# A fused block on one core: state space matrices kept to each group's 16 channels, their matmuls as pairs of 64x64 quadrants, and fold blocks formed two steps ahead

## The chip, the core and the metric

The kernel runs on one core of a Trainium2 chip. The metric is the device time of one execution in microseconds (us). The engines are named as the profile names them: PE (TensorE matmuls) and PEld (its weight loads), DVE (VectorE), ACT (ScalarE), POOL (GpSimd) and SP (SyncE), which issues the large loads.

## The reference, cut to what matters

Two transformer blocks run one after the other on 256 tokens of width 1024 (the second block puts 16 meta tokens ahead of them). The change touches only the state space branch of the second block (32 groups, each with 64 complex states and 16 channels), and one small preparation for the memory branch beside it:

```python
u32 = u.reshape(bn, L, SSM_GROUPS, SSM_GROUP)              # 32 groups of 16 channels
lam = lax.complex(a_re, a_im); dt = jnp.exp(log_dt)[:, None]
a_bar = jnp.exp(lam * dt)                                  # (32, 64)
b_bar = ((a_bar - 1.0) / lam)[..., None] * lax.complex(b_re, b_im)   # (32, 64, 16)
bu = jnp.einsum('blgc,gpc->blgp', u32, b_bar)
_, states = lax.associative_scan(combine, (a_seq, bu), axis=1)
y = jnp.real(jnp.einsum('blgp,gcp->blgc', states, c)) + d * u32
# memory branch: q, k, v = block-diagonal 4x4 maps of xc and xm, then
gates = jnp.concatenate([q, k, v], axis=-1) @ w_if + b_if
```

## The kernel before, in words

The weights come in 468 units of 512 KB (eight tiles of 128x128). SP loads a unit into one of four buffers `wr`; ACT rounds it to `wh` (L339) and DVE forms the rest `wl` (L340), up to three units ahead of PE. PE then does three fast matmuls a tile (`mm3`, L409 to L411). A step of the first block's feed-forward layer, `up(i)` and `down(i)`, takes three units. Its product of gate and value runs on POOL (L1927) after ACT and DVE have filtered what `up(i)` left in PSUM (L1923 to L1926).

Beside that stream run generators (`K.bg`). At each new unit `tick` lets every generator go one step, as far as its credit lasts. So a step that a generator yields costs one unit of the stream, whatever it holds. The scheduler then puts each engine's instructions in order; `K.paced()` lets an instruction of POOL come only after the newest feed-forward product.

`_prep` is such a generator, and runs during the feed-forward layer. It prepares the state space branch in chunks of four time steps:

- `paced` forms the matrices `bx`, `c0` and `cx` on POOL, with complex multiplications of six operations each (L577). There are eight of them: three for `bx`, one for `c0`, four for `cx`. Groups stand in pairs `q` (16 of them), 64 states of each on a half of the partitions. Each matrix has 32 columns a time step, of which a group uses its own 16 and the other 16 are zero.
- `inputs` turns `bx` into `ew` on PE (`pt`, L606), 4 at a time, copied by ACT (L607). It multiplies `bx` by `c0` into `pk` (L614), adds the direct term `d` on DVE (L620, L621), and puts the blocks of the result at their places in `tz` with ten small transfers that ACT issues (L626).
- After the powers of `a_bar` (DVE, L564 to L569) comes the fold: for each `e` in 8, POOL forms three blocks in the one buffer `ex` (`expand`, L504), and one step later PE multiplies them by the gate weights (`pf`, L657).

`_block2` runs the branch: `us` is written to DRAM and read back as `u4` with four transfers (L746), `pe` multiplies it by `ew` (L755), DVE scans, `py` forms the outputs from `tz`, `u4`, `cx` and `z2` (L793, L795), and the result goes through DRAM again (L804, four transfers). All of these matmuls are in plain float32: one such instruction leaves two records in the trace.

Of the kernel before, what the change touches and what calls it, by code (L numbers as in the profile page):

```python
# [18 lines left out]
P = 128  # L19
# [145 lines left out]
def _s5_layout(one):  # L165

    lam = np.stack([one("ssm_a_re_2"), one("ssm_a_im_2"), np.repeat(one("ssm_log_dt_2")[:, None], 64, 1)])
    lam = lam.reshape(3, 16, P).transpose(2, 0, 1).reshape(P, 48)
    bp, cp = np.zeros((P, 2, 16, 32), np.float32), np.zeros((P, 2, 16, 32), np.float32)
    for i, z in enumerate(("re", "im")):  # L170
        b, c = one(f"ssm_b_{z}_2"), one(f"ssm_c_{z}_2")
        for g in range(32):
            q, e = g // 2, g % 2
            bp[e * 64:(e + 1) * 64, i, q, e * 16:(e + 1) * 16] = b[g]
            cp[e * 64:(e + 1) * 64, i, q, e * 16:(e + 1) * 16] = c[g].T
    d = np.tile(one("ssm_d_2").reshape(16, 32).T, (4, 1))
    return np.concatenate([lam, bp.reshape(P, -1), cp.reshape(P, -1), d], 1)
# [302 lines left out]
def _prep(K, dump):  # L480
# [6 lines left out]
    ew = EW.a(16, 2, P)  # L487
    cx = [CX.a(16, 4, 32) for _ in range(2)]
    tz = TT.a(16, P)
# [19 lines left out]
    raw = ZZ.t[:, 0:2112]  # L509
    nc.scalar.dma_start(raw, I["s5p"])  # L510
    lr, li, ld = raw[:, 0:16], raw[:, 16:32], raw[:, 32:48]
    B = raw[:, 48:1072].rearrange("p (a b c) -> p a b c", a=2, b=16)
    C = raw[:, 1072:2096].rearrange("p (a b c) -> p a b c", a=2, b=16)
    dd = raw[:, 2096:2112]
    nc0, dk = (raw[:, 48 + 512 * i:560 + 512 * i].rearrange("p (a b) -> p a b", a=16) for i in range(2))
    x1, x2, kk = (ZZ.t[:, 2112 + 512 * i:2624 + 512 * i].rearrange("p (a b) -> p a b", a=16) for i in range(3))
    c0 = [TT.t[:, 2048 + 512 * i:2560 + 512 * i].rearrange("p (a b) -> p a b", a=16) for i in range(2)]
    sc = TT.t[:, 3568:4096].rearrange("p (a b) -> p a b", b=16)
    bx = [BX.a(16, 4, 32) for _ in range(2)]
# [51 lines left out]
    def paced(dr, di, xr_, xi, yr, yi):  # L571

        ops = []
        cmul(dr, di, xr_, xi, yr, yi, x1, x2, lambda *z: ops.append(z))
        for n, z in enumerate(ops):
            with K.paced():
                g.tensor_tensor(*z)  # L577
            if n not in (0, 3):
                yield 0.1

    bc = lambda z: _bc(z, 2, 32)
# [18 lines left out]
    def inputs():  # L600

        for i in range(2):
            for q4 in range(4):
                pt = K.ps("pt")
                for j in range(4):
                    tp(pt[:, j * P:(j + 1) * P], bx[i][:, 4 * q4 + j].rearrange("p a b -> p (a b)"), K.ident)  # L606
                nc.scalar.copy(ew[:, 4 * q4:4 * q4 + 4, i], pt.rearrange("p (a b) -> p a b", a=4))  # L607
                yield 0.1

        pk = K.ps("pk")  # L610
        for q in range(16):
            o = pk[:, q * 32:q * 32 + 32]
            for i in range(2):
                mm(o, bx[i][:, q].rearrange("p a b -> p (a b)"), (c0[0], nc0)[i][:, q], start=i == 0, stop=i == 1)  # L614
            if q % 4 == 3 and q < 15:
                yield 0.1
        nc.scalar.copy(kk, pk.rearrange("p (a b) -> p a b", a=16))
        yield 0.1
        lo = slice(96, 128)
        tt(dk[lo], _bc(K.ident[lo, 96:128], 1, 16), _bc(dd[lo], 2, 32), ALU.mult)  # L620
        tt(kk[lo], kk[lo], dk[lo], ALU.add)  # L621
        yield 1.2
        for t in range(4):
# [38 lines left out]
def _block2(K, X, eps, dump, stop):  # L662
# [62 lines left out]
    for n in range(4):  # L725
# [7 lines left out]
        if n >= 2:  # L733
# [3 lines left out]
            wait = []  # L737
    def ssm():
# [1271 lines left out]
```

## Time and profile before

| | |
|---|---|
| three runs, median | 1557.08 us (1553.6 to 1557.94) |
| profiled execution, its own time | 1555.69 us |
| its span in the trace | 1553.9 us |
| PE busy | 1523.9 us, 98% of the span |
| DVE, ACT, POOL busy | 1163.0, 832.5, 250.5 us |
| mean granted PE clock | 0.994 |
| HBM traffic | 164 GB/s over the span |

The span runs from the first to the last instruction that the profiler saw; 1.8 us of the execution's own time lie outside it. A busy PE is a PE with at least one matmul in flight, since matmuls overlap; how long a group of them holds the stream is read from the starts of what stands ahead of it and behind it. A granted clock of 1.00 is 2.4 GHz, and a matmul stream at the lower level runs at 1.2 GHz.

### The profile page before, as it was taken

The numbers are of one execution on the slowest core, as the hardware profiler recorded it, in microseconds if no ns is written. First come the engines' busy times: TensorE is split into PE (matmuls) and PEld (weight loads), VectorE is DVE, ScalarE is ACT, GpSimd is POOL, SyncE is SP. The second block draws the span as 40 slices with busy tenths as digits, with TensorE's granted clock in tenths as the row PEclk, the third lists the DMA queues.
The fourth block names the chain that finished last, engine by engine and source line by source line (L and its number), as shares of the span: only waits on it lengthen the run. The fifth ranks groups of instructions, "written<-read, shape, count | busy, mean of one in ns | idle before, by whom it ended". The sixth has DMA issues, their size and how long they took to land.

```text
span 1553.9 us, 29821 instructions
## 1 busy us (share of the span) xinstructions
PE 1523.9 (98%) x11693; PEld 1416.5 (91%) x11693; DVE 1163.0 (75%) x2168; ACT 832.5 (54%) x1441; POOL 250.5 (16%) x255
## 2 busy tenths in 40 slices
PE   9999999999989999999999999999999999999998
PEld 7999899999979988989999999999999888888886
DVE  6765667897866698478999888888999666665664
ACT  7764355764435557565454554554445555555554
POOL 1000000189641010001101520112222000000000
PEclk9999999999989999999999999999999999999999
DMA  7543245554545453346455455445545666656653
GB/s 269 162 136 124 96 135 186 190 186 156 153 147 164 137 162 127 105 136 207 146 177 190 151 176 189 156 160 162 163 163 165 201 193 195 195 191 192 197 194 110
DMA packets 81149, 258.09 MB, mean 166 GB/s; under 512 B 17520, under 2 KB 19312, under 8 KB 80752
## 3 DMA queue, kind: packets, MB, share of 16 engines
q1 hardware_dynamic: 69344, 247.32, 49.3%
q10 hardware_dynamic: 11664, 8.86, 1.9%
q8 instruction: 92, 1.51, 0.4%
q14 instruction: 49, 0.40, 0.1%
HBM read 253.36 MB, written 2.13 MB: 164 GB/s over the span
## 4 chain that ended last, share of the span: by engine, by line
PE 78%; DVE 11%; POOL 4%; issue 2%; ACT 2%; DMA 1%; SPq 0%; ACTq 0%; DVEq 0%; POOLq 0%
PE acc L1316 22%; PE U L409 6%; PE U L411 6%; PE U L410 6%; DVE wl L340 5%; PE g L409 3%; PE g L411 3%; PE g L410 3%; PE pG L1196 2%; POOL s L577 2%; DVE s L771 1%; PE u L409 1%; PE u L410 1%; PE u L411 1%; ACT wh L339 1%
## 5 line engine op out<-in xcount | busy, mean ns | idle before, releaser
L340 DVE TENSOR_TENSOR wl<-wr,wh 128x1024 fp32r<-128x1024 f32 (+1 forms) x469 | 595.2, 1272 | 199.5 <-ACT wh L339 196.2
L339 ACT CAST wh<-wr 128x1024 fp32r<-128x1024 f32 (+1 forms) x469 | 490.4, 1048 | 394.7 <-PE U L410 156.0
L1316 PE MATMUL acc<-wh,wring 128*128 128x512 f32 x1024 | 315.5, 389 | 0.0
L409 PE MATMUL U<-hh,wh 128*128 128x256 f32 x1024 | 292.5, 286 | 0.0
L411 PE MATMUL U<-hh,wl 128*128 128x256 f32 x1024 | 288.1, 281 | 1.5 <-DVE wl L340 1.4
L410 PE MATMUL U<-hl,wh 128*128 128x256 f32 x1024 | 288.3, 282 | 0.0
L1316 PEld LDWEIGHTS acc<-wh,wring 128*128 128x128 f32 x1024 | 192.2, 188 | 39.8
L1316 PE MATMUL acc<-wl,wring 128*128 128x512 f32 x512 | 199.2, 389 | 0.0
L411 PEld LDWEIGHTS U<-hh,wl 128*128 128x128 f32 x1024 | 193.9, 189 | 1.9 <-DVE wl L340 1.9
L409 PEld LDWEIGHTS U<-hh,wh 128*128 128x128 f32 x1024 | 193.4, 189 | 0.0
L410 PEld LDWEIGHTS U<-hl,wh 128*128 128x128 f32 x1024 | 192.5, 188 | 0.0
L1307 ACT ACTIVATE wring<-act 128x256 fp32r<-128x256 f32 x128 | 53.3, 418 | 150.5 <-PE acc L1316 147.0
L1316 PEld LDWEIGHTS acc<-wl,wring 128*128 128x128 f32 x512 | 96.1, 188 | 20.0
L1308 DVE SCALAR_TENSOR_TENSOR wring<-act,wring 128x256 fp32r<-128x256 f32 x128 | 54.7, 428 | 60.7 <-PE acc L1316 58.7
L409 PE MATMUL u<-hh,wh 128*128 128x256 f32 x320 | 92.4, 290 | 1.4 <-DVE ffn L1925 1.2
L411 PE MATMUL u<-hh,wl 128*128 128x256 f32 x320 | 91.4, 287 | 0.8 <-DVE wl L340 0.8
L410 PE MATMUL u<-hl,wh 128*128 128x256 f32 x320 | 91.4, 287 | 0.0
L1277 POOL TENSOR_TENSOR act<-act,ga 128x16 f32<-128x16 f32 (+31 forms) x77 | 56.1, 728 | 212.8 <-ACT ga L1276 190.2
L456 POOL TENSOR_TENSOR sq<-sq,sq 128x256 f32<-128x256 f32 x18 | 16.0, 888 | 402.6 <-ACT sq L452 402.4
L409 PE MATMUL g<-hh,wh 128*128 128x256 f32 x256 | 73.8, 288 | 0.0
L410 PE MATMUL g<-hl,wh 128*128 128x256 f32 x256 | 72.0, 281 | 0.0
L411 PE MATMUL g<-hh,wl 128*128 128x256 f32 x256 | 71.9, 281 | 0.0
(640 smaller groups left out, 3397.3 us busy)
## 6 DMA issues: line engine op xcount, KB each, us to landing
wr<-in_W SPq DMA_DIRECT2D x211, 512.0 KB, 3.8
wr<-in_U SPq DMA_DIRECT2D x128, 512.0 KB, 3.8
wr<-in_V SPq DMA_DIRECT2D x128, 512.0 KB, 4.3
s<-in_s5p ACTq DMA_DIRECT2D x1, 1056.0 KB, 5.0
tkc<-in_keysT ACTq DMA_DIRECT2D x1, 1024.0 KB, 6.5
wsA<-in_cst ACTq DMA_DIRECT2D x1, 804.0 KB, 6.9
wsA<-in_rows ACTq DMA_DIRECT2D x1, 640.0 KB, 5.6
s<-s ACTq DMA_DIRECT2D x10, 64.0 KB, 4.2
```

Source lines behind the costliest of these rows:

```text
L339: a = nc.scalar.copy(hi[:, q], raw[:, q])
L340: b = nc.vector.tensor_tensor(lo[:, q], raw[:, q], hi[:, q].bitcast(F32), ALU.subtract)
L409: mm(out, wh, ah, start=first, stop=False)
L410: mm(out, wh, al, start=False, stop=False)
L411: self.last = mm(out, wl, ah, start=False, stop=last).ins
L456: self.nc.gpsimd.tensor_tensor(self.part[0], self.part[0], s, ALU.add)
L577: g.tensor_tensor(*z)
L1196: mm(o, ring[:, q % 2, e // 2, :, e % 2], ring[:, q % 2, 4 + 2 * w + e // 2, :, e % 2], start=w == 0, stop=w == 1)
L1277: g.tensor_tensor(d[:, :n], d[:, :n], a[:, :n], ALU.mult)
L1307: act(hi, w, AF.Copy, scale=1.0 / 16384)
L1308: stt(lo, w, 1.0 / 16384, hi.bitcast(F32), ALU.mult, ALU.subtract)
L1316: mm(acc[t][c], w[:, q], v[:, 4 * c:4 * c + 4].rearrange("p a b -> p (a b)"), start=False, stop=i == NE - 1 and len(vs) == 1, skip_group_c ...
```

## The change

Each group's matrices keep 16 columns a time step, and each half of the partitions holds its own group's. So `bx`, `cx`, `c0` and everything that POOL computes of them are half as wide, and the packed load `s5p` has 1328 columns and not 2112. A matmul over a pair of groups becomes two over 64 partitions and 64 outputs each: lower half to lower half, upper to upper. The transposes `pt` now give 64 partitions, and two ACT copies take each to its half. The direct term comes ready for use from the host (`dk`), so one DVE addition takes `pk` from PSUM and replaces an ACT copy and two DVE operations. There are 20 small transfers into `tz` where there were ten, in four steps of 8, 6, 4 and 2; `u4` and the way back take eight each where they took four. A complex multiplication yields three times and not four. The fold forms its blocks in three buffers `exs` in turn, and PE's `pf` of step `e` stands two steps behind the blocks.

```diff
@@ _s5_layout @@
-    bp, cp = np.zeros((P, 2, 16, 32), np.float32), np.zeros((P, 2, 16, 32), np.float32)
...
+    pair = lambda z: z.reshape(16, P, 16).transpose(1, 0, 2)
+    b = np.stack([pair(one(f"ssm_b_{z}_2")) for z in ("re", "im")], 1)
...
@@ _prep @@
-    cx = [CX.a(16, 4, 32) for _ in range(2)]
-    tz = TT.a(16, P)
+    cx = [CX.a(16, 4, 16) for _ in range(2)]
+    tz = TT.a(16, 64)
...
-    bx = [BX.a(16, 4, 32) for _ in range(2)]
+    bx = [BX.a(16, 4, 16) for _ in range(2)]
+    halves = slice(0, 64), slice(64, 128)
+    exs = [BX.a(3, P) for _ in range(3)]
...
             with K.paced():
                 g.tensor_tensor(*z)
-            if n not in (0, 3):
+            if n % 2:
                 yield 0.1
...
-                    tp(pt[:, j * P:(j + 1) * P], bx[i][:, 4 * q4 + j].rearrange("p a b -> p (a b)"), K.ident)
-                nc.scalar.copy(ew[:, 4 * q4:4 * q4 + 4, i], pt.rearrange("p (a b) -> p a b", a=4))
+                    tp(pt[:64, j * P:(j + 1) * P], bx[i][:, 4 * q4 + j].rearrange("p a b -> p (a b)"), K.ident)
+                v = pt[:64].rearrange("p (a e b) -> p a e b", a=4, e=2)
+                for e, z in enumerate(halves):
+                    nc.scalar.copy(ew[z, 4 * q4:4 * q4 + 4, i], v[:, :, e])
...
             for i in range(2):
-                mm(o, bx[i][:, q].rearrange("p a b -> p (a b)"), (c0[0], nc0)[i][:, q], start=i == 0, stop=i == 1)
+                for z in halves:
+                    mm(pk[z, q * 16:q * 16 + 16], bx[i][z, q].rearrange("p a b -> p (a b)"), (c0[0], nc0)[i][z, q],
+                       start=i == 0, stop=i == 1)
...
-        nc.scalar.copy(kk, pk.rearrange("p (a b) -> p a b", a=16))
-        yield 0.1
-        lo = slice(96, 128)
-        tt(dk[lo], _bc(K.ident[lo, 96:128], 1, 16), _bc(dd[lo], 2, 32), ALU.mult)
-        tt(kk[lo], kk[lo], dk[lo], ALU.add)
+        tt(kk, pk[:, :256].rearrange("p (a b) -> p a b", a=16), dk, ALU.add)
         yield 1.2
         for t in range(4):
             for m in range(4 - t):
-                b = 3 - m
-                nc.scalar.dma_start(tz[32 * t:32 * t + 32, :, 32 * (t + m):32 * (t + m) + 32], kk[32 * b:32 * b + 32])
+                for z in (0, 64):
+                    b = z + 16 * (3 - m)
+                    nc.scalar.dma_start(tz[z + 16 * t:z + 16 * t + 16, :, 16 * (t + m):16 * (t + m) + 16], kk[b:b + 16])
+            yield 0.1
...
-    for e in range(8):
-        with K.paced():
-            for i in range(3):
-                expand(tr[i], e, ex[:, i])
+    for n in range(10):
+        if n < 8:
+            with K.paced():
+                for i in range(3):
+                    expand(tr[i], n, exs[n % 3][:, i])
         yield 0.3
+        if n < 2:
+            continue
+        e = n - 2
         pf = K.ps("pf")
         for i in range(3):
-            for q in (slice(0, 64), slice(64, 128)):
-                mm(pf[q, i // 2 * 8:i // 2 * 8 + 8], ex[q, i, q], wif[q, 8 * i + e], start=i != 1, stop=i != 0)
+            for q in halves:
+                mm(pf[q, i // 2 * 8:i // 2 * 8 + 8], exs[e % 3][q, i, q], wif[q, 8 * i + e], start=i != 1, stop=i != 0)
...
@@ _block2 @@
-        for t in range(4):
-            nc.scalar.dma_start(u4[32 * t:32 * t + 32].rearrange("c (n r) j -> c n r j", r=4), d[t])
+        for e in range(2):
+            for t in range(4):
+                z = 64 * e + 16 * t
+                nc.scalar.dma_start(u4[z:z + 16].rearrange("c (n r) j -> c n r j", r=4), d[e, t])
...
-                    mm(p[:, (i * n + j) * 68:(i * n + j + 1) * 68], ew[:, q + j, i], u4[:, q + j], start=True, stop=True)
+                    for z in halves:
+                        mm(p[z, (i * n + j) * 68:(i * n + j + 1) * 68], ew[z, q + j, i], u4[z, q + j], start=True, stop=True)
...
-                mm(o, tz[:, q], u4[:, q, 4:], start=True, stop=False)
+                for z in halves:
+                    mm(o[z], tz[z, q], u4[z, q, 4:], start=True, stop=False)
                 for i in range(2):
-                    mm(o, cx[i][:, q].rearrange("p a b -> p (a b)"), z2[:, i, q, 3:67], start=False, stop=i == 1)
+                    for z in halves:
+                        mm(o[z], cx[i][z, q].rearrange("p a b -> p (a b)"), z2[z, i, q, 3:67], start=False, stop=i == 1)
...
```

The scheduler's order shows what this moves. In PE's order the stream of unit matmuls is the same; the first `pt` stands 96 of them (four units) earlier, and the first `pf` 48 (two units) earlier. Line numbers of the changed kernel are not those of before: its L338 is L339 of before, L408 to L410 are L409 to L411, L503 is L504, L662 is L657, L765 is L755 and L1941 is L1927.

The first place is POOL's order at the end of `_prep`, from the sign change of `cx` (L598) on. Before (`ffn` is the product, `ml_3403<-ml_3403` the blocks of the fold):

```order
L598 TENSOR_SCALAR s_3399<-s_3399 128x2048
L1927 TENSOR_TENSOR ffn_3005<-ffn_3005 128x256
L504 TENSOR_TENSOR ml_3403<-ml_3403 128x128 x6
L1927 TENSOR_TENSOR ffn_3005<-ffn_3005 128x256
L504 TENSOR_TENSOR ml_3403<-ml_3403 128x128 x9
L1927 TENSOR_TENSOR ffn_3005<-ffn_3005 128x256
L504 TENSOR_TENSOR ml_3403<-ml_3403 128x128 x12
```

The same place in the changed kernel:

```order
L598 TENSOR_SCALAR s_3399<-s_3399 128x1024
L1941 TENSOR_TENSOR ffn_3005<-ffn_3005 128x256 x3
L503 TENSOR_TENSOR s_3402<-ml_3403 128x128 x9
L503 TENSOR_TENSOR ml_3403<-ml_3403 128x128 x2
L1941 TENSOR_TENSOR ffn_3005<-ffn_3005 128x256
L503 TENSOR_TENSOR s_3402<-ml_3403 128x128 x9
L1941 TENSOR_TENSOR ffn_3005<-ffn_3005 128x256
L503 TENSOR_TENSOR s_3402<-ml_3403 128x128 x6
```

Three products, and no other work, now stand between the state space matrices and the fold; the blocks of three steps stand behind one product, and PE asks for the first of them three units after the generator issued it.

The second place is ACT's order where the blocks go into `tz` (`s_3400<-s_3401`). Before:

```order
L617 COPY s_3401<-pk_4649 128x512
L626 DMA s_3400<-s_3401 32x16x32 x2
L1923 ACTIVATE ffn_3005<-u_4771,cols 128x256
L339 CAST wh_4857<-wr_4689 128x1024
L626 DMA s_3400<-s_3401 32x16x32
L1923 ACTIVATE ffn_3005<-u_4772,cols 128x256
L1926 ACTIVATE ffn_3005<-ffn_3005 128x256
L626 DMA s_3400<-s_3401 32x16x32 x7
L339 CAST wh_4900<-wr_4735 128x1024
```

In the changed kernel:

```order
L338 CAST wh_4727<-wr_4523 128x1024
L626 DMA s_3400<-s_3401 16x16x16 x8
L1937 ACTIVATE ffn_3005<-u_4725,cols 128x256
L338 CAST wh_4769<-wr_4574 128x1024
L626 DMA s_3400<-s_3401 16x16x16 x6
L1937 ACTIVATE ffn_3005<-u_4726,cols 128x256
L1940 ACTIVATE ffn_3005<-ffn_3005 128x256
L440 CAST ffnr_3006<-ffn_3005 128x256
L338 CAST wh_4812<-wr_4625 128x1024
L626 DMA s_3400<-s_3401 16x16x16 x4
L338 CAST wh_4848<-wr_4680 128x1024
L626 DMA s_3400<-s_3401 16x16x16 x2
```

Twice as many transfers of half the partitions and half the columns stand there, with one cast of weights between each two groups of them.

The third place is PE's order at the first `pe`, in the stream of `xm`. Before:

```order
L411 MATMUL xm_6291<-hi_5881,wl_6215 128x272
L409 MATMUL xm_6336<-hi_5881,wh_6255 128x272
L755 MATMUL pe_6298<-s_3400,s_3398 128x68 x6
L755 MATMUL pe_6343<-s_3400,s_3398 128x68 x6
L410 MATMUL xm_6336<-lo_5882,wh_6255 128x272
```

In the changed kernel:

```order
L410 MATMUL xm_6343<-hi_5929,wl_6263 128x272
L765 MATMUL pe_6350<-s_3400,s_3398 64x68
L765 MATMUL pe_6401<-s_3400,s_3398 64x68
L408 MATMUL xm_6394<-hi_5929,wh_6307 128x272
L765 MATMUL pe_6350<-s_3400,s_3398 64x68 x11
L765 MATMUL pe_6401<-s_3400,s_3398 64x68 x11
L409 MATMUL xm_6394<-lo_5930,wh_6307 128x272
```

Twelve instructions became 24 over 64 outputs, and the first of each of the two groups stands one `xm` matmul ahead of the rest.

## Rows read from the trace of the kernel before

**Rows 1.** The page's first part: busy us, share of the span, instructions, by engine.

```profile
PE 1523.9 (98%) x11693; PEld 1416.5 (91%) x11693; DVE 1163.0 (75%) x2168; ACT 832.5 (54%) x1441; POOL 250.5 (16%) x255
```

**Rows 2.** PE's waits in the whole span: us in total, times, longest us.

```profile
PE pf L657 <- POOL ml L504: 7.4, 5, 5.1
...
PE u L409 <- DVE ffn L1925: 1.2, 2, 0.7
PE pt L606 <- ACT s L607: 1.1, 1, 1.1
```

**Rows 3.** PE's timeline, two waits: start us, length us, instructions, idle before.

```profile
419.07 0.39 PE L1941 MATMUL acc<-ffnr,wl 128*128 128x256 f32 x1 [1.09 <-DVE wl L340]
...
438.35 0.39 PE L657 MATMUL pf<-ml 64*64 64x8 f32 x4 [5.10 <-POOL ml L504]
```

**Rows 4.** POOL's timeline: an operation of `bx`, and the product ahead of the fold.

```profile
346.30 2.16 POOL L577 TENSOR_TENSOR s<-s 128x512 f32<-128x512 f32 x1
...
436.03 0.73 POOL L1927 TENSOR_TENSOR ffn<-ffn 128x256 f32<-128x256 f32 x1 [5.22 <-DVE s L566]
```

**Rows 5.** Stretches: us, PE busy (instructions), granted PE clock, DMA share, GB/s.

```profile
435.00:440.00 5.00, 1.40 (x13) 0.71 0.57 168
440.00:445.00 5.00, 5.00 (x36) 0.61 0.47 161
...
464.00:468.00 4.00, 4.00 (x24) 0.57 0.32 114
```

**Rows 6.** PE's timeline: groups of `pt`, `pk`, `pe` and `py`, and what follows.

```profile
358.01 0.60 PE L606 MATMUL pt<-eye,s 128*128 128x128 f32 x4
...
387.29 1.87 PE L614 MATMUL pk<-s,s 128*128 128x32 f32 x16
388.99 0.36 PE L409 MATMUL u<-hh,wh 128*128 128x256 f32 x1
...
540.06 2.79 PE L755 MATMUL pe<-s,s 128*128 128x68 f32 x24
542.65 0.37 PE L410 MATMUL xm<-lo,wh 128*128 128x272 f32 x1
...
633.79 0.33 PE L793 MATMUL py<-s 128*128 128x64 f32 x2
...
639.07 0.36 PE L409 MATMUL g<-hi,wh 128*128 128x256 f32 x1
```

**Rows 7.** PE's timeline: 64x64 quadrants of the first block.

```profile
108.82 0.28 PE L410 MATMUL g<-hl,wh 128*128 128x256 f32 x1
108.94 0.28 PE L411 MATMUL g<-hh,wl 128*128 128x256 f32 x1
109.15 1.15 PE L1614 MATMUL py<-wsB 64*64 64x64 f32 x32
110.23 0.38 PE L409 MATMUL g<-hh,wh 128*128 128x256 f32 x1
110.45 0.28 PE L410 MATMUL g<-hl,wh 128*128 128x256 f32 x1
...
161.88 0.28 PE L1669 MATMUL py<-wsB,wsD 64*64 64x64 f32 x2
161.99 0.28 PE L1670 MATMUL py<-wsC,wsD 64*64 64x64 f32 x2
```

**Rows 8.** POOL's costliest groups, 300 to 520 us: busy us, mean ns.

```profile
L577 POOL TENSOR_TENSOR s<-s,s 128x512 f32<-128x512 f32 x28 | 41.7, 1509 | 0.6
...
L1927 POOL TENSOR_TENSOR ffn<-ffn 128x256 f32<-128x256 f32 x17 | 19.1, 1126 | 48.2 <-DVE ffn L1925 23.3 <-ACT ffn L1926 10.4 <-DVE s L526 5.7
```

**Rows 9.** Line 626's issues on ACT: duration ns min/median/max, first and last start.

```profile
L626 ACTq DMA_DIRECT2D s<-s x10: 592/654/1057, 405.3 to 414.9; - x10
```

**Rows 10.** ACT's timeline: three of the four issues into `u4`.

```profile
531.86 1.95 ACTq L746 DMA_DIRECT2D s<-du  x3
```

**Rows 11.** The page's DMA issues: transfers, KB each, median us to landing.

```profile
s<-du ACTq DMA_DIRECT2D x4, 136.0 KB, 4.0
```

More of the change, by code (lines that the diff above doesn't have):

```diff
@@ L168, in _s5_layout @@
     lam = lam.reshape(3, 16, P).transpose(2, 0, 1).reshape(P, 48)
-    bp, cp = np.zeros((P, 2, 16, 32), np.float32), np.zeros((P, 2, 16, 32), np.float32)
[L170 to L177, printed above, removed]
+    pair = lambda z: z.reshape(16, P, 16).transpose(1, 0, 2)
+    b = np.stack([pair(one(f"ssm_b_{z}_2")) for z in ("re", "im")], 1)
+    c = np.stack([pair(one(f"ssm_c_{z}_2").transpose(0, 2, 1)) for z in ("re", "im")], 1)
+    d = np.zeros((2, 4, 16, 16, 16), np.float32)
+    k = np.arange(16)
+    d[:, 3, k, :, k] = one("ssm_d_2").reshape(16, 2, 16).transpose(2, 1, 0)
+    return np.concatenate([lam, b.reshape(P, -1), c.reshape(P, -1), d.reshape(P, -1)], 1)
 def _ml_layout(one):
@@ L486, in _prep @@
     EW, CX, TT, ZZ, BX = (K.big(f"s5{i}") for i in range(5))
-    ew = EW.a(16, 2, P)
-    cx = [CX.a(16, 4, 32) for _ in range(2)]
-    tz = TT.a(16, P)
+    ew = EW.a(16, 2, 64)
+    cx = [CX.a(16, 4, 16) for _ in range(2)]
+    tz = TT.a(16, 64)
     u4 = TT.a(16, 68)
@@ L507, in _prep @@
     K.mlf = TT, M5, mp, nqk, wv, fold, ex, expand
-    raw = ZZ.t[:, 0:2112]
+    raw = ZZ.t[:, 0:1328]
     nc.scalar.dma_start(raw, I["s5p"])
     lr, li, ld = raw[:, 0:16], raw[:, 16:32], raw[:, 32:48]
[L512 to L517, printed above, removed]
+    B = raw[:, 48:560].rearrange("p (a b c) -> p a b c", a=2, b=16)
+    C = raw[:, 560:1072].rearrange("p (a b c) -> p a b c", a=2, b=16)
+    dk = raw[:, 1072:1328].rearrange("p (a b) -> p a b", a=16)
+    x1, x2, kk, nc0 = (ZZ.t[:, 2112 + 256 * i:2368 + 256 * i].rearrange("p (a b) -> p a b", a=16) for i in range(4))
+    c0 = [TT.t[:, 2816 + 256 * i:3072 + 256 * i].rearrange("p (a b) -> p a b", a=16) for i in range(2)]
     sc = TT.t[:, 3568:4096].rearrange("p (a b) -> p a b", b=16)
-    bx = [BX.a(16, 4, 32) for _ in range(2)]
+    bx = [BX.a(16, 4, 16) for _ in range(2)]
+    halves = slice(0, 64), slice(64, 128)
+    exs = [BX.a(3, P) for _ in range(3)]
     g.memset(tz, 0.0)
@@ L577, in paced @@
                 g.tensor_tensor(*z)
-            if n not in (0, 3):
+            if n % 2:
                 yield 0.1
-    bc = lambda z: _bc(z, 2, 32)
+    bc = lambda z: _bc(z, 2, 16)
     bar, bai = bc(ar), bc(ai)
@@ L737, in _block2 @@
             wait = []
+    halves = slice(0, 64), slice(64, 128)
     def ssm():
@@ L743, in ssm @@
         yield 0.1
-        d = du.rearrange("(r c) (n t j) -> t c n r j", r=4, n=4, t=4)
-        for t in range(4):
-            nc.scalar.dma_start(u4[32 * t:32 * t + 32].rearrange("c (n r) j -> c n r j", r=4), d[t])
+        d = du.rearrange("(r e c) (n t j) -> e t c n r j", r=4, e=2, n=4, t=4)
+        for e in range(2):
+            for t in range(4):
+                z = 64 * e + 16 * t
+                nc.scalar.dma_start(u4[z:z + 16].rearrange("c (n r) j -> c n r j", r=4), d[e, t])
         yield 0.1
@@ L801, in ssm @@
         yt = yv.rearrange("p n (t j) -> p n t j", t=4)
-        d = dy.rearrange("(t c) (n r j) -> r c n t j", t=4, n=4, r=4)
+        d = dy.rearrange("(e t c) (n r j) -> r e c n t j", e=2, t=4, n=4, r=4)
         for r in range(4):
-            nc.scalar.dma_start(yt[32 * r:32 * r + 32], d[r])
+            for e in range(2):
+                z = 32 * r + 16 * e
+                nc.scalar.dma_start(yt[z:z + 16], d[r, e])
         yield 0.1
```

1 line of the change is left out of this document (removed).

## The prediction

> **What bounds the kernel now.** I read the busy times first. PE has a matmul in flight for 98% of the span, and no other engine passes 75% [rows 1]. So the time is PE's stream plus what makes it stand still, and an edit counts if it shortens a group of PE's matmuls, ends a PE wait, or raises PE's clock. The waits come next: the longest of the program is `pf` on the blocks that POOL forms, 7.4 us in five waits, and two smaller ones lie in the same feed-forward stretch, 1.2 us for DVE and 1.1 us for an ACT copy [rows 2]. The timeline then shows where: 5.10 us end at 438.35, where the fold begins [rows 3]. It also shows who is late: the product that POOL must do before the blocks ran at 436.03, held by DVE in the powers of `a_bar`, so POOL is only the last link [rows 4]. The stretches show a second price of the wait: behind it the granted clock is 0.71 and 0.61, and 0.57 near 465, behind another `pf` wait. A mean like that is a mixture of 1.2 and 2.4 GHz [rows 5].
>
> **What the quadrants are worth on PE.** What a group costs is read from its first start to the start of what follows [rows 6]. A `pk` group takes 1.70 us, and there are four: 6.8 us. A `pe` group of 24 records takes 2.59 us, 108 ns a record; 64 records make 6.9 us. Half of `py` takes 5.28 us, both 10.6 us. Together 24.3 us for 224 records.
>
> The change doubles the records to 448, each over 64 partitions and 64 outputs. The first block has that form already: 32 records of alternating quadrants, 64 columns each, take 1.08 us from 109.15 to 110.23, 34 ns a record [rows 7]. `py` has 64 columns too, `pe` 68, `pk` only 16; I take 34 for all: 15.1 us. Coming and going is not free: the steps into the group and out of it are 0.21 and 0.22 us where the stream's pitch is 0.12 [rows 7], so 0.19 us a visit. There are twelve (four `pk`, two `py`, six `pe`, since one `xm` matmul now stands inside its first group): 2.3 us. In all 17.4 us for 24.3: **-6.9 us**. The ends: -9.2 if a visit costs nothing, and +2.6 if the halves do not overlap. That pitch is on the page of rows too: two records of one and the same quadrant take 0.11 us, 55 ns each [rows 7], and 448 of them 24.6 us, with the visits 26.9.
>
> On the visits the Trainium skill speaks against the change: its page "TensorEngine Tiling (Array Packing)", section "Key Properties", says that a change of tiling mode, and not merely of tile, drains the engine. Rows 7 agree, with the 0.21 and 0.22 us; the page gives no price, so by it the sum would be no other.
>
> The transposes `pt` keep their number and their 128 columns, and get 64 outputs. No row has that form: I take nothing, with 8 x 0.19 = 1.5 us as the upper end. Their eight further ACT copies fall to an engine that is idle 46% of the time; uncovered they would be 8 x 0.58 us (ACT's mean instruction, 832.5 / 1441 [rows 1]) = 4.6 us.
>
> **What the fold two steps ahead is worth.** A unit of the stream is 24 matmuls at 0.12 us, 2.9 us. In the changed order `pf` stands three units, 8.6 us, behind the issue of its blocks, where it stood one behind. A product as late as the one at 436.03, by 5.22 us [rows 4], still leaves 3.4 us for the blocks. I take all of the wait away: **-7.4 us**; the other end is that the 5.10 us stay.
>
> The clock goes with it. A granted mean g stands for a share 2 x (1 - g) at the lower level: 2.9 of the five us to 440, 3.9 of those to 445, 3.4 of the four to 468 [rows 5]. In the first stretch PE worked only 1.40 us. Work of 1.4 + 3.9 + 3.4 us at half the clock would take half as long: 4.3 us lost, and I take **-4 us**, with 0 as the other end.
>
> **What POOL's halving is worth.** The 48 operations on 512 columns, 28 of them at 1509 ns in the mean, become 256 wide, for which the product's row has 1126 ns [rows 8]. That is some 0.4 us each, 18 us in all, in an engine through which every product must pass. PE does not wait for it directly, so it pays only through the small waits, 1.2 + 1.1 us [rows 2]; I take half, **-1.2 us** (0 to -2.3). The order asks something back: `pt` comes four units, 11.5 us, earlier. Before, the half of `bx` that the first `pt` reads was done at 348.5 [rows 4], 9.5 us ahead of that `pt` at 358.01 [rows 6]. Its fifteen operations at 0.4 us less each end 6 us earlier, so PE should find it done with 4 us to spare. At unchanged durations 2 us would be missing, and that is the end.
>
> **What the added transfers cost.** ACT issues each piece for `tz`, and while it issues, no cast of weights runs. Ten took 654 ns each in the median [rows 9], 6.5 us, and soon after the last of them PE stood 1.09 us for weights [rows 3]: some 5.4 us of issuing were covered. Twenty pieces of a quarter of the elements lie between two bounds. If the time of an issue halves, nothing is added, and if pieces in smaller bunches fit between casts, the 1.1 us go away too: -1.1. If each takes as long as before, 13.1 - 5.4 = 7.7 us of standing, **+6.6** over before. They go out in four bunches with a cast between each two, so more is covered; nearer to the lower bound I take **+2 us**.
>
> For `u4` ACT issues eight and not four, 0.65 us each [rows 10]. Before, the last began at 533.2 and, at 4.0 us to landing [rows 11], was there at 537.2, 2.9 us ahead of the first `pe` at 540.06 [rows 6]. Four more take 2.6 us of that: just in time, **+0.5 us** (0 to 3). Queued behind them on ACT are the convolution's scalings and a cast. The way back, L804, is late by as much; PE's list of waits has none for it [rows 2], and I take nothing, with 2.6 us as the end.
>
> **The sum.** -6.9 - 7.4 - 4 - 1.2 + 2 + 0.5 = -17.0 us, from the profiled execution's 1555.69 to 1538.7. The median of the runs shown is 1557.08, 1.4 above that execution, so against it **1540 us**.
>
> **The rivals.** (1) *The fold still waits*: the product is later than its three units, since DVE's powers are moved as well and may lie upon another product. PE then stands the 5.1 us and loses half of 1.4 + 3.9 us to the clock, 2.7: -17 + 7.8 = -9.2, 1548 us. For it speaks that the wait's origin, DVE, is not touched; against it, that no work but products now stands ahead of the blocks. (2) *The halves take turns*: at 55 ns a record -17 + 6.9 + 2.6 = -7.5, 1549.6 us. Against it stand the 34 ns of the same form. The Trainium skill's rule for it is on the same page, "Gotcha 1: PSUM Pressure": different row tiles cannot access one PSUM bank at once, and here both halves of each pair write to one bank. By that rule this rival's time is the forecast; the trace does not bear it out, since the pairs of L1614 also write to one bank. (3) *Casts late by the full price of the pieces*: +6.6 and not +2 gives 1545 us. (4) *Slower*: each piece waits until the one ahead has landed. At the 4.0 us that `u4`'s pieces take [rows 11] twenty hold ACT for 80 us; less the 5.4 covered and the 1.1 of before that is +73.5, and with the other terms 1612 us. This decides from about 1.5 us a piece: the other terms sum to -19.0, so slower by 4.7 us (0.3%) needs 24.8 us of standing, 30 us of issuing. The longest of the ten took 1.06 us [rows 9]. (5) *No change*: PE's time is given back as waits on DVE, busy 75% [rows 1]; 1557 us.
>
> **How the numbers follow.** Forecast 0.68 (its own range 1533 to 1546), rival (1) 0.11, (2) 0.06, (3) 0.08, (4) 0.03, (5) 0.04. The good ends of all terms (-9.2, -7.4, -4.3, -2.3, -1.1, 0) give 1533, the low end; 1550 takes in rivals (1) to (3). About 0.3%, 4.7 us, is what a measurement of this kernel can tell from no change. Cases (1) to (3) lie below 1552.4, so faster has 0.68 + 0.25 less 0.03 for several bad ends together: 0.90; within 0.3% 0.06; slower 0.04.
>
> **What would show it.** Right: `pf` without waits and a granted clock of 1.00 through the fold; `py` in two runs of about 3.4 us, `pk` groups near 1.3; POOL's L577 near 1.1 us; at most some 3 us of standing for weights behind the `tz` pieces. Wrong: records of the quadrants 55 ns apart; the clock at its lower level behind `py`, whose quadrants work longer in one run than any before; a `pe` that waits for `u4`; longer ACT issues than 0.65 us.

## The result, and the profile after

The changed kernel takes **1535.28 us** (median of 4 runs, 1533.93 to 1536.93), the kernel before, on the same chip, 1557.51 us (median of 4, 1553.6 to 1558.68). The ratio is 0.9861, 95% interval 0.9842 to 0.9881: 22.2 us less. A second measurement, beside the experiments, gave 0.987 (0.9856 to 0.9885). The time lies in the range of the prediction and 4.7 us below its forecast of 1540. The profiled execution after took 1533.93 us, with a span of 1532.1 where it was 1553.9.

The page's first part after, which answers to [rows 1]:

```profile
PE 1510.7 (99%) x11917; PEld 1403.0 (92%) x11917; DVE 1142.1 (75%) x2167; ACT 833.8 (54%) x1448; POOL 220.1 (14%) x255
```

PE is still the bound. Its waits from 300 to 520 us come next (columns as in [rows 2]):

```profile
PE u L410 <- DVE wl L339: 0.8, 1, 0.8
PE pm L1980 <- DVE msum L1978: 0.8, 1, 0.8
PE us L408 <- ACT r2b L720: 0.7, 1, 0.7
PE acc L1955 <- DVE wl L339: 0.5, 1, 0.5
```

The `pf` wait of 7.4 us, the 1.1 us of `pt` and the 1.2 us of `u` on `ffn` [rows 2] are all gone. The stretches of the fold, and the one that answers to the last of [rows 5] (us, busy time of PE, PEld, DVE, ACT and POOL, then granted clock, DMA share, GB/s):

```profile
430.00:440.00 10.00, 10.00 (x107) 9.54 (x106) 5.93 (x9) 4.70 (x10) 5.42 (x11) 1.00 0.46 161
440.00:445.00 5.00, 5.00 (x58) 4.69 (x57) 2.77 (x5) 2.30 (x5) 0.00 (x0) 1.00 0.41 145
464.00:468.00 4.00, 4.00 (x36) 4.00 (x35) 2.66 (x4) 2.56 (x4) 0.00 (x0) 1.00 0.58 195
```

The granted clock is 1.00 in all of them. PE's timeline has the groups (answers to [rows 6]):

```profile
372.14 0.28 PE L410 MATMUL u<-hh,wl 128*128 128x256 f32 x1
372.35 1.11 PE L616 MATMUL pk<-s,s 64*64 64x16 f32 x32
373.39 0.38 PE L1953 MATMUL acc<-ffnr,wh 128*128 128x256 f32 x1
...
526.32 0.93 PE L765 MATMUL pe<-s,s 64*64 64x68 f32 x24
527.18 0.39 PE L408 MATMUL xm<-hi,wh 128*128 128x272 f32 x1
...
616.54 0.33 PE L804 MATMUL py<-s 64*64 64x64 f32 x4
...
619.49 0.38 PE L408 MATMUL g<-hi,wh 128*128 128x256 f32 x1
```

A `pk` group takes 1.04 us from its first start to the start of what follows, where it took 1.70; 24 records of `pe` take 0.86 us; half of `py`, 96 records, takes 2.95 us, 31 ns a record, where it took 5.28. POOL's groups, 300 to 520 us (answers to [rows 8]), and the issues of the pieces of `tz` (answers to [rows 9]):

```profile
L577 POOL TENSOR_TENSOR s<-s,s 128x256 f32<-128x256 f32 x28 | 28.6, 1031 | 1.0
L577 POOL TENSOR_TENSOR s<-s 128x256 f32<-128x256 f32 x20 | 20.0, 1003 | 1.3
```

```profile
L626 ACTq DMA_DIRECT2D s<-s x20: 592/621/727, 386.2 to 400.2; - x20
```

POOL's operations with two inputs fell from 1509 to 1031 ns, the other 20 from 1760 to 1003. The issues did not fall with the size: 621 ns in the median for a quarter of the elements, where 654 was the price. One place gave something back, the gates of the second block (PE's timeline):

```profile
584.51 0.28 PE L409 MATMUL g<-lo,wh 128*128 128x256 f32 x1
587.03 0.64 PE L885 MATMUL pf<-GR,ml 8*4 8x272 f32 x2 [2.24 <-DVE GR L882]
...
588.19 0.41 PE L409 MATMUL g<-lo,wh 128*128 128x256 f32 x1
588.41 0.41 PE L410 MATMUL g<-hi,wl 128*128 128x256 f32 x1
```

The wait was 0.84 us before and is 2.24 now, and behind it thirteen matmuls follow at 0.21 us instead of 0.12.

**Where the 22 us are.** I take for each group what it holds the stream: from the start of the stream's last matmul ahead of it to the first behind it, in the two traces.

| us held, or lost | before | after | difference | forecast |
|---|---|---|---|---|
| `pk` (4), `pe`, `py` | 7.3 + 7.5 + 10.8 | 5.0 + 6.4 + 6.3 | -7.9 | -6.9 |
| `pf` of the fold, its waits in it | 14.9 | 5.3 | -9.7 | -7.4 |
| matmuls at the lower clock near 442 and 466 | 3.3 | 0 | -3.3 | -4 |
| waits in and beside the `pt` groups | 3.0 | 0 | -3.0 | -1.2 |
| `acc` and its weights behind the `tz` pieces | 1.2 | 0 | -1.2 | +2 |
| `pe` and `u4` | 0 | 0 | 0 | +0.5 |
| gates: wait, and clock behind it | 0.8 | 3.5 | +2.7 | 0 |
| `pm` on `msum` | 0.3 | 1.3 | +1.0 | 0 |

They sum to -21.4; the spans differ by 21.8, of which 0.5 lie ahead of anything that the change touches. The wait of `pm` is not a fixed cost: a second trace of the changed kernel has none.

### The profile page after: what moved, and what is told of

It is laid out like the page before. It is cut to its first block, busy times and chain, and to the rows that moved or that the text cites. A ratio compares the mean times of both kernels' runs of the same rounds, so it can differ in the third digit from the quotient of the medians.

```text
span 1532.1 us, 30292 instructions
## 1 busy us (share of the span) xinstructions
PE 1510.7 (99%) x11917; PEld 1403.0 (92%) x11917; DVE 1142.1 (75%) x2167; ACT 833.8 (54%) x1448; POOL 220.1 (14%) x255
## 4 chain that ended last, share of the span: by engine, by line
PE 88%; DVE 6%; POOL 2%; ACT 2%; issue 1%; DMA 1%; SPq 0%; DVEq 0%; ACTq 0%; POOLq 0%
PE acc L1330 23%; PE U L408 6%; PE U L410 6%; PE U L409 6%; PE g L408 3%; PE g L410 3%; PE g L409 3%; PE u L408 3%; PE u L409 3%; PE u L410 3%; PE pG L1210 2%; DVE wl L339 2%; PE acc L1953 1%; PE acc L1955 1%; PE acc L1954 1%; PE q L409 1%
## 5 line engine op out<-in xcount | busy, mean ns | idle before, releaser
L339 DVE TENSOR_TENSOR wl<-wr,wh 128x1024 fp32r<-128x1024 f32 (+1 forms) x469 | 585.0, 1250 | 197.5 <-ACT wh L338 194.8
L338 ACT CAST wh<-wr 128x1024 fp32r<-128x1024 f32 (+1 forms) x469 | 490.5, 1048 | 393.4 <-PE U L409 157.1
L408 PE MATMUL U<-hh,wh 128*128 128x256 f32 x1024 | 292.5, 286 | 0.0
L410 PE MATMUL U<-hh,wl 128*128 128x256 f32 x1024 | 288.1, 281 | 1.4 <-DVE wl L339 1.4
L409 PE MATMUL U<-hl,wh 128*128 128x256 f32 x1024 | 288.3, 282 | 0.0
L410 PEld LDWEIGHTS U<-hh,wl 128*128 128x128 f32 x1024 | 193.9, 189 | 1.8 <-DVE wl L339 1.8
L408 PEld LDWEIGHTS U<-hh,wh 128*128 128x128 f32 x1024 | 193.5, 189 | 0.0
L409 PEld LDWEIGHTS U<-hl,wh 128*128 128x128 f32 x1024 | 192.5, 188 | 0.0
L408 PE MATMUL u<-hh,wh 128*128 128x256 f32 x320 | 90.7, 285 | 0.2 <-ACT hh L440 0.2
L410 PE MATMUL u<-hh,wl 128*128 128x256 f32 x320 | 89.6, 281 | 0.8 <-DVE wl L339 0.8
L409 PE MATMUL u<-hl,wh 128*128 128x256 f32 x320 | 89.6, 281 | 0.0
L408 PE MATMUL g<-hh,wh 128*128 128x256 f32 x256 | 73.8, 288 | 0.0
L409 PE MATMUL g<-hl,wh 128*128 128x256 f32 x256 | 72.0, 281 | 0.0
L410 PE MATMUL g<-hh,wl 128*128 128x256 f32 x256 | 71.9, 281 | 0.0
```

What stands on the lines that cost most here:

```text
L338: a = nc.scalar.copy(hi[:, q], raw[:, q])
L339: b = nc.vector.tensor_tensor(lo[:, q], raw[:, q], hi[:, q].bitcast(F32), ALU.subtract)
L408: mm(out, wh, ah, start=first, stop=False)
L409: mm(out, wh, al, start=False, stop=False)
L410: self.last = mm(out, wl, ah, start=False, stop=last).ins
```

## The experiments

All medians are of the kernel named; ratios are to the kernel before, run beside it on the same chip (its medians there: 1555.96 to 1556.36 us). The changed kernel was run once more beside runs 5, 7 and 11:

> The changed kernel as it is, beside the three others on one chip: 1535 us (1533.5 to 1537) by every theory.

It took 1535.56 us; this is the second measurement named above.

**1. The changed kernel with the fold as it was.**

```diff
-    for n in range(10):
-        if n < 8:
-            with K.paced():
-                for i in range(3):
-                    expand(tr[i], n, exs[n % 3][:, i])
+    for e in range(8):
+        with K.paced():
+            for i in range(3):
+                expand(tr[i], e, ex[:, i])
         yield 0.3
-        if n < 2:
-            continue
-        e = n - 2
```

> The changed kernel with its fold as it was before: one buffer, each step's matmuls right behind its blocks. Theory A (two steps ahead are what took the fold's waits and the lower clock away): pf waits 4 to 8 us in all, the granted clock falls below 0.9 somewhere between 425 and 470 us, and the time is 1544 us (1541 to 1549). Rival B (POOL's narrower work and its earlier place already make the blocks early enough): pf waits under 1.5 us, clock 1.00, 1535 us.

1548.66 us, ratio 0.9948 (0.9929 to 0.9966): 13.4 us over the changed kernel. PE's waits (first), and a stretch with the columns as above:

```profile
PE pf L657 <- POOL ml L503: 5.3, 5, 1.6
```

```profile
419.00:424.00 5.00, 5.00 (x27) 4.98 (x25) 2.10 (x4) 0.17 (x1) 2.07 (x3) 0.50 0.67 206
```

The fold's groups hold 13.3 us, 8.1 more than in the changed kernel, and some 37 matmuls at 0.21 us in place of 0.12 lose another 3.4. Theory A holds; rival B falls. The wait is now five waits of at most 1.6 us, and not one of 5.1. In POOL's timeline the blocks come right behind products that had themselves waited 4.4 to 6.1 us, for DVE or PE; so product and blocks stand in it together, and the run does not part them.

**2. The kernel before with the fold two steps ahead alone** (the reverse edit, with two more block buffers).

> The kernel before with the fold two steps ahead and nothing else of the change. Theory A: pf waits under 1 us, the pitch of the feed-forward matmuls stays at 0.12 us behind the fold, and the time falls by the wait of 7.4 us and up to 4 us of clock: 1546 to 1550 us. Rival B (the product that comes ahead of the blocks is as late as before, so that the wait stays): over 1553 us with pf waits over 4 us. If the parts simply add, the gains of this run and of e1_fold_one_step sum to the 22 us of the whole change.

1550.76 us, ratio 0.9962 (0.9947 to 0.9978): a gain of 5.2 us, just short of what A expected. And the gains of runs 1 and 2, 7.3 and 5.2 us, do not sum to 22. PE's waits, then DVE's and POOL's timelines, and a stretch:

```profile
PE u L409 <- DVE ffn L1930: 3.5, 3, 2.4
...
PE pf L662 <- DVE ffn L1930: 0.7, 1, 0.7
```

```profile
425.29 3.60 DVE L565 TENSOR_TENSOR s<-s 128x16 f32<-128x16 f32 x1
```

```profile
424.25 6.34 POOL L599 TENSOR_SCALAR s<-s 128x2048 f32<-128x2048 f32 x1
```

```profile
445.00:450.00 5.00, 3.88 (x18) 3.92 (x19) 3.52 (x7) 1.78 (x4) 3.89 (x6) 0.50 0.64 203
```

`pf` waits 0.7 us, as forecast. But PE has only moved on to the next thing that is late: `u` waits 3.5 us for DVE's convolution, and the clock falls to 0.50, the 1.2 GHz level, behind it. One DVE operation on 16 columns took 3.60 us (its like take 0.17) while POOL ran its negation of 2048 columns, 6.34 us by the trace.

**3. Run 2 with that one negation on ACT.**

```diff
-            g.tensor_scalar(cx[1], cx[1], -1.0, None, ALU.mult)
+            act(cx[1], cx[1], AF.Copy, scale=-1.0)
```

> The kernel before with the fold two steps ahead, and the one negation of 2048 columns (6.34 us on POOL) done on ACT. Theory A (that POOL instruction holds a DVE operation on 16 columns for 3.60 us, DVE's queue is late by as much, and u then waits 3.5 us for DVE): u's waits on ffn fall under 1 us, the pitch stays at 0.12 us at 446 to 451 us, and the time falls from 1550.8 to 1545 us (1543 to 1547.5). Rival B (the 64 small operations of the powers alone make DVE late): u still waits 3 us or more, 1550 us.

1545.94 us, ratio 0.9926 (0.9911 to 0.9942): 4.8 us from one instruction. ACT's timeline, and PE's wait:

```profile
421.79 1.92 ACT L599 ACTIVATE s<-s 128x2048 f32<-128x2048 f32 x1 [1.51 <-POOL s L578]
```

```profile
PE u L409 <- DVE ffn L1930: 1.9, 3, 0.8
```

No DVE operation on 16 columns takes over 1.2 us any more, and the clock of 445 to 450 us is 1.00. A holds, though 1.9 us of the wait stay, more than the 1 us I allowed. The edit frees DVE of that hold and POOL's queue of 6.34 us at once, and does not part the two. The Trainium skill has the rule, on its page "SBUF — State Buffer", section "SBUF: two separate sides": of a GpSimd operation that reads SBUF and a DVE operation with two SBUF inputs, the one that starts first has a shared port pair for its whole instruction, and the other stands. The trace of run 2 agrees in kind, with 3.60 us beside the long instruction and 0.17 without it, but not in extent: the DVE operation ended at 428.89, 1.7 us ahead of the end recorded for POOL's, and the next two took their usual 0.16 and 1.21 us (spans on POOL are rough).

**4. Run 2 with POOL's products, and its negation, on half the columns.**

```diff
-    bc = lambda z: _bc(z, 2, 32)
+    bc = lambda z: _bc(z, 2, 16)
...
+        ops = [tuple(y[..., :16] if hasattr(y, "shape") else y for y in z) for z in ops]
```

> The kernel before with the fold two steps ahead and POOL's products on 16 of the 32 columns of each pair (the other half of bx, c0 and cx is left at zero, so the state space matrices of half the channels are left out; PE's matmuls are as before). Theory A (narrower POOL work is what gives DVE its time back): pt waits and u's waits go, DVE's longest operation on 16 columns stays under 2 us, and the time is 1543 us (1541 to 1546). Rival B (the narrow work is worth only the place it frees on POOL, for which PE does not wait): 1550 us.

1539.92 us, ratio 0.9892 (0.9875 to 0.9908): 10.8 us below run 2, with PE's matmuls as in the kernel before. DVE's split of weights, 316 to 400 us, and ACT's wait for POOL's product, 316 to 430 us, first in run 2 and then here:

```profile
L340 DVE TENSOR_TENSOR wl<-wr,wh 128x1024 fp32r<-128x1024 f32 x27 | 45.0, 1678 | 1.6 <-ACT wh L339 1.3
```

```profile
ACT ffnr L441 <- POOL ffn L1932: 19.6, 10, 3.5
```

```profile
L340 DVE TENSOR_TENSOR wl<-wr,wh 128x1024 fp32r<-128x1024 f32 x29 | 39.8, 1374 | 11.9 <-ACT wh L339 11.9
```

```profile
ACT ffnr L441 <- POOL ffn L1935: 13.2, 10, 3.6
```

Beside wide POOL products a split takes 1678 ns in the mean, beside narrow ones 1374, and DVE, which was never idle for long, now waits 11.9 us for ACT. No `pt` group holds the stream over 0.48 us, `u` no longer waits for `ffn`, and no DVE operation on 16 columns takes over 1.03 us. A's signs are all there, and the time lies below its range: this is the largest single part of the change. Between 316 and 520 us the two traces differ by 9.6 us: 3.2 at the `pt` groups, 1.3 at the weights behind the `tz` pieces, most of the rest at `u` and in the clock behind it. Elsewhere two things cancel: this version has two more memsets on POOL, for the zero halves, and PE loses some 3 us near 305 us, soon after the last of them; and run 2's trace has a stretch at the lower clock near 663 us, some 3 us, that this one has not.

**5. The changed kernel with each product issued twice.**

```diff
             with K.paced():
-                g.tensor_tensor(*z)
+                for _ in range(2):
+                    g.tensor_tensor(*z)
```

> The changed kernel with each of POOL's 48 products issued twice, so that POOL's work is about as long as before the change, at the new place. Theory A (POOL's products slow DVE's operations beside them, and this, not POOL's own end, cost PE its waits): DVE's wl in the stretch 316 to 400 us goes from 1.40 back towards 1.68 us in the mean, pt or u wait some 3 us or more, and the time is 1543 us (1539 to 1550). Rival B (only the width of single products matters, because DVE is held by one long instruction at a time): wl rises, but no new PE wait over 1 us, 1535 to 1537 us.

1557.75 us, ratio 1.0001 (0.9991 to 1.0011): the time of before. PE's waits, 316 to 430 us, and ACT's:

```profile
PE pt L607 <- ACT s L610: 4.5, 2, 4.1
PE u L410 <- DVE wl L339: 4.3, 3, 3.2
PE u L408 <- DVE ffn L1940: 2.4, 2, 1.9
PE pt L607 <- DVE ffn L1940: 2.3, 1, 2.3
PE pt L607 <- POOL s L578: 1.6, 1, 1.6
```

```profile
ACT ffnr L440 <- POOL ffn L1942: 40.0, 7, 7.1
```

The doubled products are busy for 86.9 us, where those of before were for 76.8 and the changed kernel's are for 48.6, and PE asks for `pt` four units earlier than before. So this run asks more of POOL than the kernel before did, and that it lands on the same time is chance. The waits are larger than A forecast, and one of 1.6 us is for POOL's product itself, which A had ruled out. The mark that A named was wrong too: `wl` stays at 1374 ns in the mean (31.4 us for 23), so narrow products do not slow the splits more for being twice as many. What grows is the other path: the feed-forward's product stands behind them in POOL's queue, and ACT, which must round it (`ffnr`), waits 40.0 us for POOL where the changed kernel has 12.2. The next casts of weights stand behind that in ACT's queue. So POOL reaches PE in two ways: through its queue, as here, and beside wide instructions by slower operations on DVE, as runs 2 to 4 show; how much PE pays for the second alone no run shows.

**6. The changed kernel at the old pace** (`if n not in (0, 3)` for `if n % 2`).

> The changed kernel with the products given out as before, four steps a product of complex numbers and not three, so that pt comes some 3 units later and everything behind it too. Theory A (the place is worth little, the widths do it): 1535 us (1533.5 to 1537), pf waits under 1 us. Rival B (the earlier place is what lets DVE be done with the powers before the fold): waits of pt, u or pf of 3 us or more and a lower clock behind them, 1540 us or more.

1538.23 us, ratio 0.9886 (0.987 to 0.9902), 2.9 us over the changed kernel: between the two theories. No `pt` or `pf` waits, so the widths do most; but PE's waits, and the stretch behind them, show

```profile
PE u L410 <- DVE wl L339: 2.6, 2, 1.8
```

```profile
416.00:424.00 8.00, 7.12 (x47) 7.12 (x48) 7.86 (x18) 5.06 (x8) 4.67 (x2) 0.79 0.39 134
```

The longest of these waits comes at 416.88, behind the `tz` pieces, whose last issue starts at 413.42: the weights were cast by 414.14, and DVE split them at 415.61, behind a convolution for which ACT, after that issue, had the input ready at 414.55. That these are the +2 us of the prediction is read from the place, not tested. At the new pace the same twenty issues meet other work and cost PE nothing.

**7. The changed kernel with 40 pieces for `tz`** (each cut in two along the pairs).

> The changed kernel with each of the 20 transfers of tz cut in two, so that ACT issues 40. Theory A (an issue takes some 0.62 us whatever it carries, and ACT has cover for 20 of them but not for 40): 12.4 us more of issuing, waits of u or acc for wl or wh of 3 to 9 us between 390 and 425 us, perhaps a lower clock behind them, and the time is 1542 us (1538 to 1549). Rival B (ACT has cover enough): 1535 us.

1548.31 us, ratio 0.9951 (0.9938 to 0.9964), 13 us more. ACT's issues; PE's waits; a stretch:

```profile
L627 ACTq DMA_DIRECT2D s<-s x40: 592/611/1883, 386.8 to 414.3; - x40
```

```profile
PE u L408 <- ACT wh L338: 5.3, 2, 3.0
PE u L410 <- DVE wl L339: 2.3, 3, 0.8
```

```profile
400.00:416.00 16.00, 11.38 (x58) 10.68 (x59) 10.71 (x46) 4.20 (x8) 0.77 (x1) 0.68 0.36 85
```

Theory A holds, near its upper end. Twenty more issues at 0.61 us are 12.2 us, and the time rose by 13, but not one for one: between 398 and 416 us PE stood 6.8 us for weights, and 36 matmuls at the lower clock lost another 3.4. So twenty were covered, forty are not, and some 5 us of the additional issuing still were.

**8. The changed kernel without alternating halves.** In each group the records of one half stand ahead of those of the other.

```diff
-            for j in range(8):
-                q = 8 * h + j
-                o = p[:, j * 64:(j + 1) * 64]
-                for z in halves:
+            for z in halves:
+                for j in range(8):
+                    q = 8 * h + j
+                    o = p[:, j * 64:(j + 1) * 64]
...
```

> The changed kernel with all records of one half of pk, pe and py ahead of those of the other half, within each group; the records are the same 448. Theory A (a record costs 31 to 34 ns only because consecutive records lie in different quadrants, and costs 55 ns beside one of its own quadrant): the groups take 448 x 21 to 24 ns = 9 to 11 us more, py two runs of 5 us instead of 3, and the time is 1545 us. Rival B (the cost is one of issue, whatever the quadrant): py stays at 3 us a run, 1535 us.

1541.81 us, ratio 0.9908 (0.9889 to 0.9926). PE's timeline, the first and what follows the first half of `py`:

```profile
617.27 0.33 PE L806 MATMUL py<-s 64*64 64x64 f32 x2
...
622.83 0.39 PE L408 MATMUL g<-hi,wh 128*128 128x256 f32 x1
```

5.56 us for 96 records: 58 ns each, where alternating ones take 31. `pk` goes from 32 to 55 ns, `pe` from 36 to 57. In the changed kernel's `py` the records start in pairs, the two of a pair 7 ns apart and a pair every 58 ns: two records in different quadrants cost the time of one. Without alternation the three groups hold 28.6 us, more than the 25.6 of the kernel before. The groups hold 10.9 us more in all, and A holds; the time rose by only 6.5, since the gates' wait is 0.84 us again without a lower clock behind it (2.7 us), and `pm` starts 0.25 us behind the matmul ahead of it and not 1.03 (0.8 less). About 1 us of the difference I don't place.

**9. `py`'s halves in two banks.**

```diff
-            p = K.pm_("py")
+            ps = [K.pm_("py"), K.pm_("py")]
```

> The changed kernel with py's two halves in two different PSUM banks (and the GELU as two instructions of 64 partitions). Theory A (the same bank costs the pairs nothing): py stays at 31 ns a record, 2.9 to 3.1 us a run, and the time at 1535 us, perhaps 0.5 more for the two further ACT instructions. Rival B (halves that write to one bank take turns, as the Trainium skill's page TensorEngine Tiling (Array Packing), section Gotcha 1: PSUM Pressure, says): a record falls towards half, py to some 1.5 to 2 us a run, and the time to 1533 us.

1534.59 us, ratio 0.9853 (0.9832 to 0.9874), not told apart from the changed kernel. PE's timeline, as in run 8:

```profile
617.75 0.33 PE L804 MATMUL py<-s 64*64 64x64 f32 x4
...
620.69 0.38 PE L408 MATMUL g<-hi,wh 128*128 128x256 f32 x1
```

2.94 us for 96 records, in one bank or in two. The rule of the Trainium skill ("TensorEngine Tiling (Array Packing)", "Gotcha 1: PSUM Pressure") that different row tiles cannot access one bank at once is not seen in this pitch.

**10. and 11. The gates later.** Two tries to take back the 2.24 us: a larger credit ahead of the gates' `pf`, and one more step ahead of it.

```diff
-        yield 0.4
+        yield 1.2
         pf = K.pm_("pf")
```

```diff
         yield 0.4
+        yield 0.1
         pf = K.pm_("pf")
```

> The changed kernel with 1.2 in place of 0.4 as the credit asked ahead of the gates' pf matmul (the wait on GR of 2.2 us at 585 us, behind which the pitch is 0.21 us for some 3 us). Theory A (PE reaches this matmul too early now, since it runs 20 us earlier while ACT and DVE take as long as before): the wait goes under 0.5 us, the granted clock at 585 to 592 is 1.00, and the time is 1532 us (1530.5 to 1533.5). Rival B (the steps behind it, gcol and the keys' weights, are only pushed back and wait in their turn): 1535 us or more.

> The changed kernel with one more step of the background work ahead of the gates' pf, so that this matmul stands one unit (24 matmuls, 2.9 us) later. Theory A (PE only comes too early there): the wait of 2.2 us on GR goes, and the time is 1532.5 us (1531 to 1534). Rival B (the steps behind it are on a chain of their own and wait by as much more): 1535 us or more.

The first moved nothing: every matmul stands where it stood, the wait is 2.2 us, and 1535.42 us (0.9867, 0.985 to 0.9884) are a further measurement of the changed kernel. So it tells neither theory from the other. The second took 1542.37 us (0.9906, 0.9891 to 0.992). PE's timeline:

```profile
587.25 0.61 PE L886 MATMUL pf<-GR,ml 8*4 8x272 f32 x2 [2.71 <-DVE GR L882]
...
647.30 0.58 PE L409 MATMUL gl<-s5r,wh 128*128 128x256 f32 x1 [3.22 <-DVE s5r L441]
```

The edit does not do what was expected of it: in PE's order the gates' `pf` stands one matmul later, not 24. The wait did not shrink, and the attention steps behind it came out in another order, with a new wait of 3.22 us and a lower clock at 640 to 680 us (0.79). So this run does not tell the theories apart either. Where the 2.24 us come from can be read from ACT's timeline, in the kernel before and in the changed one:

```profile
592.37 0.42 ACT L990 ACTIVATE gs<-gs 128x256 f32<-128x256 f32 x1 [1.52 <-DVE gs L989]
```

```profile
573.64 0.42 ACT L1004 ACTIVATE gs<-gs 128x256 f32<-128x256 f32 x1 [2.92 <-DVE gs L1003]
```

Ahead of the gates ACT waits 1.40 us longer for DVE, in whose queue the steps of the state space scan stand, and the gates' wait grew by the same 1.40 us. The gates' wait is 0.8 or 0.9 us in the kernel before and in runs 2, 3, 4 and 8, and 2.2 or 2.3 us in the changed kernel and in runs 1, 5, 6, 7, 9 and 10: it comes with the alternating quadrants. That PE leaves `pe` earlier while DVE's scan takes as long as before would explain it; no run tests that step. No version here beats the changed kernel.

## Why the prediction was right, and which terms were mis-sized

**Quadrants, -6.9.** Right, -7.9 measured. 34 ns a record was close for `pe` (36) and `pk` (32) and high for `py` (31), the largest group. The 0.19 us of a visit is seen again (0.21 us from 372.14 to 372.35, and 0.23 from 373.39 to the next). Run 8 shows the mechanism: it is the alternation that makes them cheap. Rival (2), halves that take turns, falls. What the term left out is that the gates' wait of +2.7 us comes with it (run 11), so that some 5 us of it are left.

**`pt`, nothing.** Right: a group without a wait holds the stream for 0.47 to 0.48 us before and after, with no price for the form of 64 outputs.

**The fold and its clock, -7.4 and -4.** The size came out, -13.0 for -11.4, but the step "I take all of the wait away" left out a condition. It asked whether the blocks would be in time, and they are: 0.7 us in run 2. It did not ask what DVE, late for another reason, would hold next. Two steps ahead alone gain 5.2 us, so that the size came out is in part luck: it needed POOL's narrower work, which the prediction priced as a small term of its own. "POOL is only the last link" misses the first link. In the trace before, one operation of DVE's powers took 3.61 us beside POOL's negation (424.46 to 430.80 us), the instruction that run 3 takes off POOL:

```profile
425.50 3.61 DVE L564 TENSOR_TENSOR s<-s 128x16 f32<-128x16 f32 x1
```

What the prediction saw as "PE's time is given back as waits on DVE", its rival (5) with a chance of 0.04, is what happens in run 2 to about half the gain, and POOL's narrower work is what prevents it in the changed kernel.

**POOL's halving, -1.2.** This term was mis-sized twice. Its work: 0.4 us for each of 48 operations, 18 us, was taken from a row of 28 of them, and the other 20 were dearer:

```profile
L577 POOL TENSOR_TENSOR s<-s 128x512 f32<-128x512 f32 x20 | 35.1, 1760 | 0.9
```

All 48 fell from 76.8 to 48.6 us. And its price: "PE does not wait for it directly, so it pays only through the small waits" counted the waits that bore POOL's name or lay beside it. Run 4 gives 10.8 us for it once the fold stands ahead, and run 3 gives 4.8 of such a gain to one instruction. Runs 2 and 4 make 16.0 us for the fold and POOL together, where the prediction had 12.6. The table books these microseconds where PE lost them, and there the missing 4.7 us are spread: 3.2 at the `tz` pieces, 1.8 at `pt`, 1.6 at the fold, 1.0 at the quadrants, 0.5 at `u4` and 0.5 ahead of the change, less 3.7 given back. The sign was in the trace before: DVE's splits took 1679 ns in the mean beside POOL's products (316 to 400 us) and 1228 nearly without them (480 to 600 us), and ACT waited 19.8 us for POOL's product.

```profile
L340 DVE TENSOR_TENSOR wl<-wr,wh 128x1024 fp32r<-128x1024 f32 x27 | 45.0, 1679 | 1.6 <-ACT wh L339 1.3
```

```profile
L340 DVE TENSOR_TENSOR wl<-wr,wh 128x1024 fp32r<-128x1024 f32 x33 | 40.5, 1228 | 9.3 <-ACT wh L339 9.0 <-PE u L410 0.4
```

What is shown is that the wide POOL work costs PE its time; how much goes by DVE's slower operations and how much by POOL's queue is not separated: run 3 takes away both at once, and run 5 shows that the queue alone can cost as much.

**The `tz` pieces, +2.** An issue came out at the dear bound (621 ns, 20 times, for 654), and the cover was larger than taken: forecast 2 us lost, measured 1.2 won. In run 4 the wait behind the pieces is gone too, with the ten pieces of before, so POOL's narrower work is enough to take it away; before, the split that this wait was for took 1.91 us. Run 6 has a loss at the old pace, 2.9 us in all, and run 7 shows that forty are not covered. Rival (3), casts late by the full price, falls, at the old pace too; rival (4), a wait for each landing, falls.

**`u4`, +0.5, and the way back, 0.** No wait for either. "Just in time" was right: the last piece was issued at 517.5 us, they took 3.0 us to landing in the median, and the first `pe` started at 520.68.

**Not foreseen: +3.7 us given back** at the gates and at `pm`. The prediction costed no wait outside the changed places. They and the gains above it hide each other in part, so that the time is nearer to the forecast than the terms are. Rival (1), the fold still waits, falls with run 2; rival (5) as an outcome of the whole change falls with the result.

## What to carry to other kernels

Before an edit on an engine "off the path" is costed at nothing, look at what its instructions do to their neighbours: compare the same operation of the busy engine beside it and without it (1.68 us against 1.23 here), and look who waits for what stands behind it in its queue. An edit that removes a wait hands PE on to the next late thing, so cost a set of such edits together and test them one by one: here two steps ahead were worth 5.2 us alone and 13.4 with the others in place. Quadrants paid here because consecutive records alternate between them: without that they cost more than the full matmuls. That both halves write to one bank cost nothing (run 9).

## What the runs showed of the hardware that was not expected

- A DVE operation on 16 columns took 3.60 us beside a POOL instruction on 2048 columns, and 0.17 us with that instruction on ACT; it ended 1.7 us ahead of the end recorded for POOL's.
- Consecutive records in one quadrant cost 55 to 58 ns, alternating ones 31 to 36, at 16, 64 and 68 columns; in `py` two alternating ones start 7 ns apart.
- A DMA issue on ACT took about 0.6 us at all three sizes of the `tz` pieces: 654, 621 and 611 ns in the median for a whole, a quarter and an eighth.
